# The starts of the stationary weights in the gate and up projections, moved chunk by chunk

## The chip, the cores and the metric

The kernel runs on one NeuronCore of one Trainium2 chip. Its time is the device time of one execution in microseconds. The time before is the median of three runs; a further execution was taken by the hardware profiler.

## What is computed

A decoder trunk of two layers over 256 tokens with a width of 1024, in float32. Each layer adds half of a SwiGLU FFN, a mixer, and half of a second FFN, each behind an RMS norm:

```python
def swiglu(x, w_gate, w_up, w_down):
    return (jax.nn.silu(x @ w_gate) * (x @ w_up)) @ w_down

for layer in range(DEPTH):          # 2
    h = h + 0.5 * swiglu(rms_norm(h, ffn1_norm[layer]), ...)
    hn = rms_norm(h, mix_norm[layer])
    h = h + (ab_mixer(hn, ...) if layer % 2 == 0 else c_mixer(hn, ...))
    h = h + 0.5 * swiglu(rms_norm(h, ffn2_norm[layer]), ...)
return rms_norm(h, final_norm)
```

The FFNs' inner width is 2816. The mixer of layer 0 is dilated window attention beside a spatial gate, that of layer 1 block-sparse attention. There are thus four FFNs, called the first to the fourth here; in the code they are phases 0, 2, 3 and 5, and phases 1 and 4 are the mixers.

## The kernel before

**Two parts of every number.** All large matrix products run in the type `F32R`. Each operand is split into its copy in that type and the rest that the copy lost, `whi` and `wlo` for weights, `xTh` and `xTl` for activations, and each product takes three matmuls: high by high, high by low, low by high.

**The stream of weights.** All weight matrices are cut into chunks of 128 x 2048 numbers. `Stream` brings them in their order of use: `load_one` starts the DMA into a `raw` buffer (3 of them), `split_parts` makes `whi` on ScalarE (L74) and `wlo` on VectorE (L75), each in two halves of 1024, and `take` hands a chunk to TensorE. There are 4 buffers for each part. A buffer has 2112 columns (`CH + LINE`), 64 more than a chunk, so that a chunk may start up to 256 bytes further on: `shift` in `Stream.add` counts columns of 4 bytes. Before the change chunks that are 256 wide start at `SHIFT`, 16 columns or 64 bytes, all others at 0.

**Where the operands lie.** In the built program `xTh` and `xTl` start at 36352 and 44544 bytes within each partition, the `whi` buffers at 170752, 179200, 187648 and 196096, the `wlo` buffers at 136960, 145408, 153856 and 162304. All these are multiples of 256, and the spacers `EDGE` and `GAP` are there in the layout. Within a chunk, each step of k is 1024 bytes and each half of the width 512 bytes further on. So the start of a stationary operand, less that of its moving operand, has one residue modulo 256 for a whole chunk and part; the text calls this residue the *distance*. Before the change it is 64 bytes for every chunk of width 256.

**An FFN.** The first 512 columns of gate and up are made in four blocks with activations as the stationary operand (`rowwise`, L199 to L201). The other 2304 columns are made by `colwise`: chunks of 256 columns, gate and up in turn, 18 chunks in each FFN. Here a 128 x 128 piece of the weights is stationary, and the 256 tokens of the activations are moving:

```python
for k in range(KD):
    h, l = w[0][:, k, cs], w[1][:, k, cs]
    nc.tensor.matmul(p, h, xh, ...)   # L322
    nc.tensor.matmul(p, h, xl, ...)   # L323
    nc.tensor.matmul(p, l, xh, ...)   # L324
```

One chunk is 2 halves of 8 steps of k, 16 such triples or 48 matmuls; one FFN is 288 triples. Between the first and the second chunk `turn_all` puts four transposes (L447); after that nothing but these triples stands on TensorE until the last chunk. Then `project` (L339, L340, L343) multiplies by the down matrix, in chunks whose start is 0. The mixers use `colwise` too, between other work, with chunks that start at 64 bytes; their attention scores (L539, L540) have `q` as the stationary and `kh` or `kl` as the moving operand, all of which start on multiples of 256.

The order on each engine is the order in which the program issues its work, apart from the tile framework's placing; the DMAs of the weights are issued from SyncE's queue.

Of the kernel before, what the change touches and what calls it, by code (L numbers as in the profile page):

```python
# [11 lines left out]
F32R = mybir.dt.float32r  # L12
# [12 lines left out]
CH = 2048  # L25
# [4 lines left out]
HEAT0 = 14  # L30


LINE, SHIFT = 64, 16
EDGE, GAP = 56, 8


class Stream:
# [4 lines left out]
        self.specs, self.raws, self.parts = [], {}, {}  # L42
        self.loaded = self.split = self.done = self.next = 0

    def add(self, src, nk, w, shift=0):
        self.specs.append((src, nk, w, 2 if len(self.specs) < 4 else 1, shift))

    def load_one(self):
# [15 lines left out]
    def split_parts(self):  # L64
        j = self.split
        nc = self.nc
        _, nk, w, cuts, shift = self.specs[j]
        n = nk * w
        raw = self.raws.pop(j)
        hi, lo = (p.tile([128, CH + LINE], F32R, name=m)[:, shift : shift + n]  # L70
                  for p, m in ((self.hi_pool, "whi"), (self.lo_pool, "wlo")))
        h = n // (2 * cuts)
        for a in range(0, n, h):
            nc.scalar.activation(hi[:, a : a + h], raw[:, a : a + h], AF.Copy)  # L74
            nc.vector.tensor_sub(lo[:, a : a + h], raw[:, a : a + h], hi[:, a : a + h].bitcast(F32))  # L75
            yield
        self.parts[j] = tuple(t.rearrange("p (k c) -> p k c", k=nk) for t in (hi, lo))
        self.split += 1
# [25 lines left out]
def trunk(ctx: ExitStack, tc: tile.TileContext, a, out):  # L104
# [15 lines left out]
    st = Stream(nc, (raw_pool, hi_pool, lo_pool))  # L120


    def add_cols(m, c0, w):
        n = CH // w
        for k in range(0, KD, n):
            st.add(m[k * 128 : (k + n) * 128, c0 : c0 + w], n, w, SHIFT if w == 256 else 0)

    def add_ffn(wg, wu, wd):
        for m in (wg, wu):
            add_cols(m, 0, 512)  # L130
        for c in range(512, FF, 256):
            for m in (wg, wu):
                add_cols(m, c, 256)
        add_rows(wd, range(0, FT, 2))

    def add_rows(m, order):
        for k in order:
            st.add(m[k * 128 : (k + 2) * 128, :], 2, D)

    add_ffn(a["ffn1_w_gate"][0], a["ffn1_w_up"][0], a["ffn1_w_down"][0])  # L140
    wab = a["ab_w_in"][0]
    add_cols(wab, 1024, 512)
    add_cols(wab, 2048, 512)
    add_cols(wab, 1536, 256)
    add_cols(wab, 1792, 256)
    for c in range(2):
        add_cols(wab, c * 256, 256)
        add_cols(wab, 512 + c * 256, 256)
    add_rows(a["ab_w_out"][0], (4, 6, 0, 2))
    add_ffn(a["ffn2_w_gate"][0], a["ffn2_w_up"][0], a["ffn2_w_down"][0])  # L150
    add_ffn(a["ffn1_w_gate"][1], a["ffn1_w_up"][1], a["ffn1_w_down"][1])
    wc = a["c_w_in"][0]
    add_cols(wc, 2048, 512)
    for c in range(4):
# [2 lines left out]
        add_cols(wc, c * 256, 256)  # L157
        add_cols(wc, 1024 + c * 256, 256)
    add_rows(a["c_w_out"][0], (0, 2, 4, 6))
    add_ffn(a["ffn2_w_gate"][1], a["ffn2_w_up"][1], a["ffn2_w_down"][1])  # L160


    def rows(v, n):
# [52 lines left out]
    class Norm:  # L216
# [8 lines left out]
        def add(self, h, bank, factor):  # L225
            sl = slice(h * 512, (h + 1) * 512)
            xs = xr[self.t][:, sl]
            if factor == 1.0:
                nc.vector.tensor_add(xs, bank, xs)
            else:  # L230
                nc.vector.scalar_tensor_tensor(xs, bank, factor, xs, op0=ALU.mult, op1=ALU.add)
# [578 lines left out]
```

## Time and profile before

| | before |
|---|---|
| runs, us | 962.03, 962.15, 965.7 (median 962.15) |
| profiled execution, us | 965.49 |
| its span, us | 963.8 |
| mean granted TensorE clock | 0.999 |
| TensorE matmuls busy, us | 951.3 (99%) |
| weight loads busy, us | 867.0 (90%) |
| VectorE busy, us | 560.6 (58%) |
| ScalarE busy, us | 523.1 (54%) |

The profiled execution is near the slowest of the three timed runs. Matmuls are pipelined, so the time that one matmul is shown with (276 ns for 256 columns) is longer than the distance from its start to the next one's; what a matmul costs is read from starts, or from counts over a stretch of time. In the names of a row, the output stands before the arrow and the operands behind it; `whi<-raw` is a split, `bank<-xTh,whi` a matmul into a PSUM bank.

### The profile page before, as it was taken

To read this page: it belongs to the slowest core of one execution; us is meant where nothing else is said; L and a number is where in the kernel's file an instruction comes from. 1 tells how busy PE (TensorE), PEld (TensorE's weight loads), DVE (VectorE), ACT (ScalarE), POOL (GpSimd) and SP (SyncE) were. 2 spreads that over 40 slices of the span, in tenths; PEclk is the share of its full clock that TensorE was granted. 3 is DMA by queue.
4 is the path that set the end of the run, shared out by engine and by line. 5 is a ranking of instruction groups with operands and counts; after the bars stand their busy time and mean duration, and the time that the engine had idled before them with its cause. 6 is when DMAs were issued, how large, how long until landed. Compare 5 with 4: busy or idle time off the path is not lost.

```text
span 963.8 us, 15449 instructions
## 1 busy us (share of the span) xinstructions
PE 951.3 (99%) x6371; PEld 867.0 (90%) x6371; DVE 560.6 (58%) x815; ACT 523.1 (54%) x875; POOL 42.0 (4%) x72
## 2 busy tenths in 40 slices
PE   9999999999999999999999999999999999999997
PEld 7999998889978999988789999888999779999885
DVE  6655544478766555454655555446788666555442
ACT  7644443476976444443654454337798775454431
POOL 0000000011200000000000000000213000000000
PEclk9999999999999999999999999999999999999999
DMA  9756555556334755555466565554543337565521
GB/s 323 246 176 204 190 186 207 175 173 223 128 130 159 234 176 179 195 195 180 154 211 198 182 212 177 202 190 142 178 170 132 131 113 259 187 206 179 208 96 44
DMA packets 119783, 174.70 MB, mean 181 GB/s; under 512 B 3952, under 2 KB 92832, under 8 KB 119712
## 3 DMA queue, kind: packets, MB, share of 16 engines
q1 hardware_dynamic: 117136, 171.48, 53.1%
q10 hardware_dynamic: 2576, 2.23, 0.8%
q8 instruction: 50, 0.82, 0.3%
q14 instruction: 21, 0.17, 0.1%
HBM read 172.65 MB, written 1.05 MB: 180 GB/s over the span
## 4 chain that ended last, share of the span: by engine, by line
PE 83%; ACT 7%; DVE 5%; issue 3%; POOL 1%; DMA 0%; POOLq 0%; SPq 0%; DVEq 0%; ACTq 0%
PE bank L322 15%; PE bank L324 15%; PE bank L323 15%; PE bank L339 9%; PE bank L343 9%; PE bank L340 9%; PE bank L199 4%; PE bank L200 4%; PE bank L201 4%; ACT whi L74 2%; DVE wlo L75 2%; ACT pr L545 1%; POOL rstd L211 1%; ACT pr L551 1%; DVE xTl L289 1%
## 5 line engine op out<-in xcount | busy, mean ns | idle before, releaser
L74 ACT ACTIVATE whi<-raw 128x1024 fp32r<-128x1024 f32 (+1 forms) x332 | 328.9, 1038 | 361.9 <-issue 230.6
L75 DVE TENSOR_TENSOR wlo<-raw,whi 128x1024 fp32r<-128x1024 f32 (+1 forms) x332 | 384.3, 1196 | 233.1 <-ACT whi L74 232.4
L322 PE MATMUL bank<-xTh,whi 128*128 128x256 f32 x1376 | 383.1, 279 | 0.0
L324 PE MATMUL bank<-xTh,wlo 128*128 128x256 f32 x1376 | 382.0, 278 | 0.0
L323 PE MATMUL bank<-xTl,whi 128*128 128x256 f32 x1376 | 382.0, 278 | 0.0
L324 PEld LDWEIGHTS bank<-xTh,wlo 128*128 128x128 f32 x1376 | 259.6, 189 | 0.1
L323 PEld LDWEIGHTS bank<-xTl,whi 128*128 128x128 f32 x1376 | 258.8, 188 | 0.2
L322 PEld LDWEIGHTS bank<-xTh,whi 128*128 128x128 f32 x1376 | 258.5, 188 | 0.3
L339 PE MATMUL bank<-whi,hTh 128*128 128x512 f32 x352 | 137.3, 390 | 0.0
L340 PE MATMUL bank<-wlo,hTh 128*128 128x512 f32 x352 | 137.0, 389 | 0.0
L343 PE MATMUL bank<-whi,hTl 128*128 128x512 f32 x352 | 113.7, 389 | 0.0
L438 DVE TENSOR_TENSOR hm<-sil,bank 128x512 f32<-128x512 f32 x44 | 30.2, 687 | 88.5 <-PE bank L324 78.2
L343 PEld LDWEIGHTS bank<-whi,hTl 128*128 128x128 f32 x352 | 66.1, 188 | 13.7
L340 PEld LDWEIGHTS bank<-wlo,hTh 128*128 128x128 f32 x352 | 66.1, 188 | 13.6
L339 PEld LDWEIGHTS bank<-whi,hTh 128*128 128x128 f32 x352 | 66.1, 188 | 13.5
L199 PE MATMUL bank<-whi,xTh 128*128 128x512 f32 x192 | 76.2, 397 | 0.1
L200 PE MATMUL bank<-wlo,xTh 128*128 128x512 f32 x192 | 75.4, 392 | 0.6 <-DVE wlo L75 0.5
L201 PE MATMUL bank<-whi,xTl 128*128 128x512 f32 x192 | 75.1, 391 | 0.0
L211 POOL TENSOR_TENSOR rstd<-ms,half_neg 128x1 f32<-128x1 f32 x14 | 12.9, 921 | 800.3 <-DVE ms L240 800.3
L200 PEld LDWEIGHTS bank<-wlo,xTh 128*128 128x128 f32 x192 | 36.1, 188 | 9.4 <-DVE wlo L75 2.5
L201 PEld LDWEIGHTS bank<-whi,xTl 128*128 128x128 f32 x192 | 36.0, 188 | 7.6
L199 PEld LDWEIGHTS bank<-whi,xTh 128*128 128x128 f32 x192 | 36.1, 188 | 7.4 <-ACT xTh L287 0.3
(91 smaller groups left out, 681.3 us busy)
## 6 DMA issues: line engine op xcount, KB each, us to landing
raw<-in_ffn_w_down SPq DMA_DIRECT2D x44, 1024.0 KB, 4.9
raw<-in_ffn_w_gate SPq DMA_DIRECT2D x42, 1024.0 KB, 5.2
raw<-in_ffn_w_up SPq DMA_DIRECT2D x42, 1024.0 KB, 5.3
raw<-in_c_w_in SPq DMA_DIRECT2D x12, 1024.0 KB, 5.2
raw<-in_ab_w_in SPq DMA_DIRECT2D x10, 1024.0 KB, 5.3
raw<-in_ab_w_out SPq DMA_DIRECT2D x4, 1024.0 KB, 5.0
raw<-in_c_w_out SPq DMA_DIRECT2D x4, 1024.0 KB, 4.8
raw<-in_ffn_w_gate SPq DMA_DIRECT2D x4, 512.0 KB, 6.5
```

The source lines that it names most:

```text
L74: nc.scalar.activation(hi[:, a : a + h], raw[:, a : a + h], AF.Copy)
L75: nc.vector.tensor_sub(lo[:, a : a + h], raw[:, a : a + h], hi[:, a : a + h].bitcast(F32))
L199: nc.tensor.matmul(p, sh, mh, start=start, stop=False)
L200: nc.tensor.matmul(p, sh, ml, start=False, stop=False)
L201: nc.tensor.matmul(p, sl, mh, start=False, stop=stop)
L322: nc.tensor.matmul(p, h, xh, start=k == 0, stop=False)
L323: nc.tensor.matmul(p, h, xl, start=False, stop=False)
L324: nc.tensor.matmul(p, l, xh, start=False, stop=k == KD - 1)
L339: nc.tensor.matmul(banks[t, h], sh, w[0][:, kw, cs], start=first, stop=False)
L340: nc.tensor.matmul(banks[t, h], sh, w[1][:, kw, cs], start=False, stop=False)
L343: nc.tensor.matmul(banks[t, h], sl, w[0][:, kw, cs], start=False, stop=last)
L438: nc.vector.tensor_mul(hm, g, pu)
```

## The change

Only the place of weight chunks inside their buffers is changed, and only for the 256-wide chunks of the four FFNs. `shift` becomes a pair, one number for `whi` and one for `wlo`. A new function `places` gives the pair for chunk `c` (0 to 17) of each FFN: `a` is a multiple of 16 bytes, 16 x (7c mod 16) in the first, third and fourth FFN and 16 x (5c mod 16) in the second, so that the chunks of an FFN pass through all 16 multiples under 256 and then repeat the first two. In the first and second FFN both parts are put at `a`; in the third `whi` stays at 64 bytes and `wlo` is put at `a`; in the fourth `whi` is put at `a` and `wlo` stays. The distances in the first, third and fourth FFN are thus, in units of 16 bytes, 0, 7, 14, 5, 12, 3, 10, 1, 8, 15, 6, 13, 4, 11, 2, 9, 0, 7, and in the second 0, 5, 10, 15, 4, 9, 14, 3, 8, 13, 2, 7, 12, 1, 6, 11, 0, 5; 4 is the distance before. The mixers' chunks stay at 64 bytes, all others at 0. Buffers keep their size and place.

```diff
+def places(ffn, c):
+    a = 4 * ((7, 5, 7, 7)[ffn] * c % 16)
+    return ((a, a), (a, a), (SHIFT, a), (a, SHIFT))[ffn]
...
-    def add(self, src, nk, w, shift=0):
+    def add(self, src, nk, w, shift=(0, 0)):
...
-        hi, lo = (p.tile([128, CH + LINE], F32R, name=m)[:, shift : shift + n]
-                  for p, m in ((self.hi_pool, "whi"), (self.lo_pool, "wlo")))
+        hi, lo = (p.tile([128, CH + LINE], F32R, name=m)[:, d : d + n]
+                  for p, m, d in ((self.hi_pool, "whi", shift[0]), (self.lo_pool, "wlo", shift[1])))
...
-    def add_cols(m, c0, w):
+    def add_cols(m, c0, w, shift=None):
         n = CH // w
         for k in range(0, KD, n):
-            st.add(m[k * 128 : (k + n) * 128, c0 : c0 + w], n, w, SHIFT if w == 256 else 0)
-
-    def add_ffn(wg, wu, wd):
+            st.add(m[k * 128 : (k + n) * 128, c0 : c0 + w], n, w, shift or ((SHIFT, SHIFT) if w == 256 else (0, 0)))
+
+    def add_ffn(i, wg, wu, wd):
         for m in (wg, wu):
             add_cols(m, 0, 512)
         for c in range(512, FF, 256):
-            for m in (wg, wu):
-                add_cols(m, c, 256)
+            for j, m in enumerate((wg, wu)):
+                add_cols(m, c, 256, places(i, (c - 512) // 128 + j))
         add_rows(wd, range(0, FT, 2))
```

The four calls of `add_ffn` pass 0 to 3 as the FFN's number.

More of the change, by code (lines that the diff above doesn't have):

```diff
@@ L138, in add_rows @@
             st.add(m[k * 128 : (k + 2) * 128, :], 2, D)
-    add_ffn(a["ffn1_w_gate"][0], a["ffn1_w_up"][0], a["ffn1_w_down"][0])
+    add_ffn(0, a["ffn1_w_gate"][0], a["ffn1_w_up"][0], a["ffn1_w_down"][0])
     wab = a["ab_w_in"][0]
@@ L149, in trunk @@
     add_rows(a["ab_w_out"][0], (4, 6, 0, 2))
-    add_ffn(a["ffn2_w_gate"][0], a["ffn2_w_up"][0], a["ffn2_w_down"][0])
-    add_ffn(a["ffn1_w_gate"][1], a["ffn1_w_up"][1], a["ffn1_w_down"][1])
+    add_ffn(1, a["ffn2_w_gate"][0], a["ffn2_w_up"][0], a["ffn2_w_down"][0])
+    add_ffn(2, a["ffn1_w_gate"][1], a["ffn1_w_up"][1], a["ffn1_w_down"][1])
     wc = a["c_w_in"][0]
@@ L159, in trunk @@
     add_rows(a["c_w_out"][0], (0, 2, 4, 6))
-    add_ffn(a["ffn2_w_gate"][1], a["ffn2_w_up"][1], a["ffn2_w_down"][1])
+    add_ffn(3, a["ffn2_w_gate"][1], a["ffn2_w_up"][1], a["ffn2_w_down"][1])
     def rows(v, n):
```

## The prediction

> **What bounds the kernel now.** I read the head of the page first, then the chain that ended last.
>
> ```profile
> span 963.8 us, 15449 instructions
> ...
> PE 951.3 (99%) x6371; PEld 867.0 (90%) x6371; DVE 560.6 (58%) x815; ACT 523.1 (54%) x875; POOL 42.0 (4%) x72
> ...
> PE 83%; ACT 7%; DVE 5%; issue 3%; POOL 1%; DMA 0%; POOLq 0%; SPq 0%; DVEq 0%; ACTq 0%
> ```
>
> TensorE is busy in 99% of the span, and the chain lies on it for 83%. No instruction is added or removed by the change, so the time can move only if single matmuls, or the splits that feed them, become longer or shorter. The profiled execution took 965.49 us for its span of 963.8 us; the three timed runs gave 962.03, 962.15 and 965.7.
>
> Next I compared stretches of the same work by counts: four stretches of 50 us, one in each FFN's `colwise` loop. Behind the stretch and its length stand each engine's busy time with its instructions (TensorE's matmuls, its weight loads, VectorE, ScalarE, GpSimd), then the granted clock, the DMA share and GB/s.
>
> ```profile
> 50.00:100.00 50.00, 50.00 (x444) 50.00 (x443) 26.42 (x27) 22.59 (x27) 0.00 (x0) 1.00 0.59 192
> 330.00:380.00 50.00, 50.00 (x427) 50.00 (x426) 26.40 (x26) 21.99 (x27) 0.00 (x0) 1.00 0.57 183
> 530.00:580.00 50.00, 50.00 (x444) 50.00 (x443) 28.13 (x29) 22.62 (x27) 0.00 (x0) 1.00 0.58 190
> 830.00:880.00 50.00, 50.00 (x444) 50.00 (x443) 27.77 (x29) 22.62 (x27) 0.00 (x0) 1.00 0.58 190
> ```
>
> The same loop does 444 matmuls in 50 us in three FFNs and only 427 in the second, at the same granted clock (1.00) and with PE busy throughout. So one and the same instruction has two lengths. The order of time shows them; a triple (L322, L323, L324) is one step of k.
>
> ```profile
> 60.49 0.28 PE L322 MATMUL bank<-xTh,whi 128*128 128x256 f32 x1
> ...
> 63.55 0.28 PE L322 MATMUL bank<-xTh,whi 128*128 128x256 f32 x1
> ...
> 340.59 0.28 PE L322 MATMUL bank<-xTh,whi 128*128 128x256 f32 x1
> ...
> 343.77 0.28 PE L322 MATMUL bank<-xTh,whi 128*128 128x256 f32 x1
> ```
>
> Nine triples lie between each pair: 3.06 us or 340 ns a triple in the first FFN (113.3 a matmul), 3.18 us or 353.3 ns in the second (117.8). I call these the low and the high level; they differ by 13.3 ns a triple. In both stretches the stationary operand starts 64 bytes behind the moving one, counted modulo 256, so at this distance both levels are possible. The line's own view, asked for each FFN from the restart after its first chunk to the end of its loop, shows how firmly a level is held (minimum, median and maximum of one matmul in ns; in the order first to fourth FFN):
>
> ```profile
> L322 PE MATMUL bank<-xTh,whi x271: 276/276/276, 40.8 to 132.6; 128*128 128x256 f32 x136
> L322 PE MATMUL bank<-xTh,whi x271: 281/281/281, 318.3 to 413.7; 128*128 128x256 f32 x136
> L322 PE MATMUL bank<-xTh,whi x270: 276/276/276, 505.9 to 597.3; 128*128 128x256 f32 x135
> L322 PE MATMUL bank<-xTh,whi x270: 276/276/276, 805.4 to 896.9; 128*128 128x256 f32 x135
> ```
>
> Each FFN has one level for some 90 us, 276 or 281 ns in a matmul's own duration. It is drawn where four transposes (L447) interrupt the loop, once in each FFN, after the first chunk; that chunk was on the high level in all four. The first chunk of the third FFN, and the restart:
>
> ```profile
> L322 PE MATMUL bank<-xTh,whi x15: 281/281/281, 499.4 to 504.4; 128*128 128x256 f32 x15
> 504.81 0.49 PE L447 MATMUL bank<-ident,hm 128*128 128x128 f32 x3
> ```
>
> I read this as two stable timings between the weight load and the running matmul, chosen by a few nanoseconds at the restart and then kept. Whether distance matters as well is told by the score matmuls (L539, L540), whose operands both start on a multiple of 256: distance 0, the same 256 columns.
>
> ```profile
> 246.84 0.28 PE L539 MATMUL bank<-kh,q 128*128 128x256 f32 x1
> ...
> 247.80 0.28 PE L322 MATMUL bank<-xTh,whi 128*128 128x256 f32 x1
> ...
> 248.16 0.28 PE L322 MATMUL bank<-xTh,whi 128*128 128x256 f32 x1
> ...
> 733.10 0.28 PE L322 MATMUL bank<-xTh,whi 128*128 128x256 f32 x1
> 733.44 0.28 PE L539 MATMUL bank<-kh,q 128*128 128x256 f32 x1
> ...
> 733.80 0.28 PE L540 MATMUL bank<-kl,q 128*128 128x256 f32 x1
> ```
>
> Eight score matmuls take 0.96 us (120 ns each). At 733 they follow a triple of 0.34 us and are at 0.12 at once: distance 0 leaves the low level whatever came before. And the triple after the eight takes 0.36 us: back at distance 64, without a stop, the high level is kept.
>
> **The change part by part.** On every engine the instructions stand in the same order with the same shapes, and all buffers lie where they lay; the DMA queue and its landings are untouched. What moves is the start of a stationary operand, by a multiple of 16 bytes: in the first two FFNs for `whi` and `wlo` of 17 of the 18 chunks (816 of 864 matmuls each), in the third for `wlo` alone (272), in the fourth for `whi` alone (544); 2448 of 3456 matmuls.
>
> *The splits.* ScalarE writes `whi` and VectorE reads it and writes `wlo` at the new starts. I cost this at nothing.
>
> ```profile
> L75 DVE TENSOR_TENSOR wlo<-raw,whi 128x1024 fp32r<-128x1024 f32 x38 | 44.8, 1221 | 24.9 <-ACT whi L74 24.9
> L74 ACT ACTIVATE whi<-raw 128x1024 fp32r<-128x1024 f32 x36 | 36.2, 1054 | 51.1 <-issue 44.0 <-PE bank L323 5.8 <-DMA raw<-in_ffn_w_up 1.4
> ```
>
> These are the groups of the first FFN's loop (34 to 133 us). A chunk is 16 triples, 5.44 us of TensorE; its splits are 2 x 1.054 on ScalarE and 2 x 1.221 on VectorE. In the 50 us stretches VectorE is busy 26 to 28 us, ScalarE 23. The cover of about 2.4 us a chunk is gone only if a split took twice as long.
>
> *The matmuls.* First the floor. In the profiled run the high level holds in the second FFN (288 triples) and in the first chunk of each other FFN (16 triples each, before the transposes): 336 x 13.3 ns = 4.5 us. With all FFNs low this execution would take 961.0 us. It stands 3.3 us over the median; the second FFN low from its restart would take 272 x 13.3 ns = 3.6 us off, so I take the two faster timed runs for the same program with that FFN settled low. The floor holds for both.
>
> All 1152 FFN triples high cost 15.4 us over the floor. In the other direction no row goes below the low level. At distance 0, 20 ns a triple over the low level is paid instead of 13.3: four chunks with both parts there and four with one, at most 0.8 us more, taken as 0.4.
>
> What share of the triples will be high? Before, each FFN drew its level once. After, there is a new distance every 5.4 us; each FFN passes distance 0 in its first chunk and again in its seventeenth (one operand of two in the last two FFNs), and distance 0 drops TensorE to the high side. Between lies only the one restart after the first chunk. The nearest rows are the mixers, where the same loop at distance 64 is entered again and again from scores and transposes. Mean durations of L323 by stage, in the order first FFN, second FFN, dilated mixer (216 to 255 us), block-sparse mixer (666 to 741):
>
> ```profile
> L323 PE MATMUL bank<-xTl,whi 128*128 128x256 f32 x288 | 79.6, 276 | 0.0
> L323 PE MATMUL bank<-xTl,whi 128*128 128x256 f32 x288 | 80.9, 281 | 0.0
> L323 PE MATMUL bank<-xTl,whi 128*128 128x256 f32 x95 | 26.4, 278 | 0.0
> L323 PE MATMUL bank<-xTl,whi 128*128 128x256 f32 x128 | 35.7, 280 | 0.0
> ```
>
> 276 is all low, 281 all high, so the mixers stand at 0.4 and 0.8, weighted (95 x 0.4 + 128 x 0.8)/223 = 0.63. I take that share for the disturbed FFN loops: 0.63 x 15.4 = 9.7 us. The bounds are 0 (every distance but 0 lets the drawn level stand) and 1 (one bad distance is enough, and nothing releases). Sum: 961.0 + 9.7 + 0.4 = 971.1, forecast 971 us.
>
> A rule of the Trainium skill speaks against all of this: its page "TensorE: Matmul & The Clock Gate", Part 2 (Step-by-step), says that TensorE has two independent read ports, so that loading the next weights takes nothing from the running matmul. By that rule the distance would be without effect and the time would stay near 962. The trace disagrees: 120 ns at distance 0 against 113.3 at 64, same columns, same clock.
>
> **The rivals.**
> 1. *The drawn level survives.* Distances other than 0 may be as neutral as 64, each FFN settles at its restart (three of four settled low in this profile) and keeps the level through sixteen chunks. For it: inside an FFN no switch of chunk changes anything before, though buffers rotate. Against it: the residue never changed there, and after 120 ns at distance 0 the high level stayed. With under 0.38 of the triples high: 961 to 966.9, so not slower by more than the bound. The rule of the two ports belongs here.
> 2. *Nothing releases.* The first bad distance puts each FFN on the high level to its end. For it: 247.80 to 248.16 above. Against: the mixers do come back, at transposes. 961.0 + 15.4 + 0.4 = 976.8; I count 975.2 to 978 to it.
> 3. *Some distances are dearer than 0.* No row shows more than 120 ns for a steady run of 256 columns, but no row has a start off a multiple of 32 either. If half the chunks paid twice the excess of distance 0 (126.7 ns, 40 ns a triple), 576 x 40 ns = 23 us, with the rest at 0.63 x 7.7 = 4.8: 989.
> 4. *Some distances are better than 64: faster.* From 0 to 64 6.7 ns went; were another 4.4 ns a matmul to go in half the chunks, 1728 x 4.4 ns = 7.6 us would leave 953.4. It decides from 0.27 of the time (961.0 to 957.3 is 3.7 us, over 15.2). Against it speak the 512-column rows:
>
> ```profile
> 146.99 0.39 PE L339 MATMUL bank<-whi,hTh 128*128 128x512 f32 x1
> 147.22 0.39 PE L340 MATMUL bank<-wlo,hTh 128*128 128x512 f32 x1
> ```
>
> 0.23 us from start to start for 512 columns, twice the low level's 0.113 for 256, though one weight load of the same 128 columns now has double the time beside it: 113.3 looks like what 256 columns cost undisturbed. The same page of the Trainium skill (Back-to-back issue gap) gives 262 cycles for 256 columns, 109.2 ns as an estimate at its 2.4 GHz; no run here shows that for this type.
>
> **How the numbers follow.** The forecast's case, a mixed share of 0.4 to 0.9 (967.1 to 975.2), has 0.42; rival 1 has 0.25, rival 2 0.20, rival 3 0.10, rival 4 0.03. A measurement of this kernel tells about 0.5% from no change, 4.8 us of 962.15: faster means under 957.3, slower over 967.0. So slower 0.42 + 0.20 + 0.10 = 0.72, same 0.25, faster 0.03. The range takes in rivals 1 and 2 down to the floor and up to the dearest sum: 961 to 978, leaving out 0.13.
>
> **What would show it right or wrong.** Right: starts of L322 that step by 340 ns in some chunks and 353 to 360 in others, changing at borders of chunks; the first and the seventeenth chunk of the first two FFNs at 360; splits of L74 and L75 still near 1054 and 1221 ns; chain on PE as before. Rival 1: 444 matmuls in 50 us in most FFNs. Rival 2: 427 or fewer in all four. Wrong altogether: steps under 340 or over 360 ns, a split twice as long, or idle time of PE ahead of L322 with `whi` or `wlo` as releaser.

## The result: 978.12 us, 1.4% slower, and the profile after

The changed kernel takes 978.12 us (median of four runs, 978.05 to 978.15), where the kernel before took 963.92 (median of four, 962.03, 962.15, 965.7 and 969.46). The ratio is 1.0143, 95% interval 1.0109 to 1.0176. The forecast was 971, the range 961 to 978, so the time lies at its upper end, 0.1 us past it. The profiled execution took 978.14 us for a span of 976.4 us; before it was 965.49 for 963.8, so 12.6 us came in.

The head of the page after, and its chain that ended last:

```profile
span 976.4 us, 15449 instructions
...
PE 963.9 (99%) x6371; PEld 879.5 (90%) x6371; DVE 560.9 (57%) x815; ACT 523.8 (54%) x875; POOL 42.0 (4%) x72
...
PE 87%; DVE 4%; ACT 4%; issue 3%; POOL 1%; DMA 0%; POOLq 0%; SPq 0%; DVEq 0%; ACTq 0%
```

TensorE's busy time went from 951.3 to 963.9 us, by the 12.6 us of the span; VectorE and ScalarE stand where they stood. Stretches of 50 us within the four `colwise` loops (the columns are as in the prediction):

```profile
50.00:100.00 50.00, 50.00 (x425) 50.00 (x424) 25.80 (x27) 22.45 (x27) 0.00 (x0) 1.00 0.60 189
335.00:385.00 50.00, 50.00 (x427) 50.00 (x426) 26.41 (x26) 21.65 (x28) 0.00 (x0) 1.00 0.60 183
530.00:580.00 50.00, 50.00 (x428) 50.00 (x427) 26.33 (x27) 22.29 (x27) 0.00 (x0) 1.00 0.61 190
830.00:880.00 50.00, 50.00 (x427) 50.00 (x427) 27.70 (x28) 22.64 (x27) 0.00 (x0) 1.00 0.60 189
```

Before, the counts were 444, 427, 444 and 444; now all four FFNs, at 425 to 428, are within two of the second one's. From start to start, the 864 matmuls of each FFN's loop add up to 98.2, 101.8, 98.2 and 98.2 us before and to 102.4, 102.3, 101.9 and 102.2 after: 12.4 of the 12.6 us. The mixers' `colwise` work, which was not changed, is at 79.2 and 79.3 us.

The splits, the groups of the whole kernel, which have moved lines (L74 and L75 are L81 and L82 now, and L322 to L324 are L329 to L331):

```profile
L82 DVE TENSOR_TENSOR wlo<-raw,whi 128x1024 fp32r<-128x1024 f32 x316 | 374.3, 1223 | 237.4 <-ACT whi L81 236.7
L81 ACT ACTIVATE whi<-raw 128x1024 fp32r<-128x1024 f32 x316 | 320.2, 1059 | 373.8 <-issue 241.6 <-PE bank L350 75.7 <-PE bank L330 28.2
```

1223 and 1059 ns: the new starts cost the splits nothing.

What the loss looks like inside an FFN is seen at chunk 12 of the first, the one that lies at 64 bytes as before, between chunk 11 (208 bytes) and chunk 13 (176 bytes). The line's own view for each of the three (minimum, median and maximum of one matmul):

```profile
L329 PE MATMUL bank<-xTh,whi x16: 276/278/279, 97.5 to 102.8; 128*128 128x256 f32 x16
L329 PE MATMUL bank<-xTh,whi x16: 276/276/287, 103.1 to 108.3; 128*128 128x256 f32 x16
L329 PE MATMUL bank<-xTh,whi x16: 278/279/283, 108.6 to 113.9; 128*128 128x256 f32 x16
```

Only chunk 12 has a median of 276 ns, the low level. By starts, the triples of these chunks take 350, 340 and 355 ns. Over all 72 chunks of the four FFNs, four run at 340: three with both parts at 64 bytes, and the one with `whi` at 64 and `wlo` at 192. The others lie between 347 and 367 ns, each with its own step; the mean over all is 355.

### The profile page after: what moved, and what is told of

It is laid out like the page before. It is cut to its first block, busy times and chain, and to the rows that moved or that the text cites. A ratio compares the mean times of both kernels' runs of the same rounds, so it can differ in the third digit from the quotient of the medians.

```text
span 976.4 us, 15449 instructions
## 1 busy us (share of the span) xinstructions
PE 963.9 (99%) x6371; PEld 879.5 (90%) x6371; DVE 560.9 (57%) x815; ACT 523.8 (54%) x875; POOL 42.0 (4%) x72
## 4 chain that ended last, share of the span: by engine, by line
PE 87%; DVE 4%; ACT 4%; issue 3%; POOL 1%; DMA 0%; POOLq 0%; SPq 0%; DVEq 0%; ACTq 0%
PE bank L330 16%; PE bank L329 16%; PE bank L331 16%; PE bank L346 9%; PE bank L350 9%; PE bank L347 9%; PE bank L206 4%; PE bank L207 4%; PE bank L208 4%; DVE wlo L82 1%; POOL rstd L218 1%; ACT whi L81 1%; DVE xTl L296 1%; ACT xn L262 1%; PE bank L284 1%
## 5 line engine op out<-in xcount | busy, mean ns | idle before, releaser
L81 ACT ACTIVATE whi<-raw 128x1024 fp32r<-128x1024 f32 (+1 forms) x332 | 329.3, 1040 | 373.8 <-issue 241.6
L82 DVE TENSOR_TENSOR wlo<-raw,whi 128x1024 fp32r<-128x1024 f32 (+1 forms) x332 | 384.4, 1197 | 238.3 <-ACT whi L81 237.5
L329 PE MATMUL bank<-xTh,whi 128*128 128x256 f32 x1376 | 386.8, 281 | 0.0
L330 PE MATMUL bank<-xTl,whi 128*128 128x256 f32 x1376 | 386.2, 281 | 0.0
L331 PE MATMUL bank<-xTh,wlo 128*128 128x256 f32 x1376 | 385.9, 281 | 0.0
L329 PEld LDWEIGHTS bank<-xTh,whi 128*128 128x128 f32 x1376 | 259.4, 189 | 0.3
L331 PEld LDWEIGHTS bank<-xTh,wlo 128*128 128x128 f32 x1376 | 259.6, 189 | 0.1
```

The lines of the kernel that those rows point to most:

```text
L329: nc.tensor.matmul(p, h, xh, start=k == 0, stop=False)
L330: nc.tensor.matmul(p, h, xl, start=False, stop=False)
L331: nc.tensor.matmul(p, l, xh, start=False, stop=k == KD - 1)
```

## The experiments

Steps below are nanoseconds per triple, from start to start of the matmuls in the trace (340 is the low level, 353 the prediction's high level). The fences show stretches of equal length, one in each FFN from the first to the fourth unless the text says otherwise; in 40 us some 356 matmuls mean a step of 340, 342 a step of 353, 336 a step of 360. A step given for an FFN or a chunk is a mean where single triples differ: at 56 bytes, for one, triples of 348 to 360 ns take turns. A pair such as (64, 192), or 64 with 192, gives the places of `whi` and `wlo` in bytes. All but the two kernels that are given with intervals ran once.

**One distance for a whole FFN.** In `places`:

```diff
-    a = 4 * ((7, 5, 7, 7)[ffn] * c % 16)
-    return ((a, a), (a, a), (SHIFT, a), (a, SHIFT))[ffn]
+    a = (48, 56, 32, 52)[ffn]
+    return a, a
```

> Both parts of all 18 chunks of an FFN at one distance, with no change inside an FFN: 192, 224, 128 and 208 bytes in the first to fourth FFN. Theory M (memory: a bad distance puts TensorE on the high level and it stays there): a constant distance other than 0 is as neutral as 64, so after the restart behind the first chunk each FFN settles at 340 ns a triple in about three cases of four; the time is 962 to 966 us. Theory D (each distance has its own step, whatever came before): the same steps as these distances had inside the changed kernel, 353, 350, 355 to 360 and 350 ns, held through the whole FFN; 288 triples each, 13 + 10 + 17 + 10 ns above 340, together about 14 us over the floor of 961: 974 to 976 us.

```profile
90.00:130.00 40.00, 40.00 (x342) 40.00 (x341) 21.69 (x22) 17.60 (x21) 0.00 (x0) 1.00 0.55 184
370.00:410.00 40.00, 40.00 (x345) 40.00 (x345) 21.77 (x23) 17.61 (x21) 0.00 (x0) 1.00 0.55 185
550.00:590.00 40.00, 40.00 (x340) 40.00 (x338) 21.12 (x22) 17.72 (x23) 0.00 (x0) 1.00 0.56 187
850.00:890.00 40.00, 40.00 (x345) 40.00 (x345) 21.70 (x22) 17.58 (x21) 0.00 (x0) 1.00 0.57 186
```

975.43 us. The steps are 353, 350, 356 and 350, much as in the changed kernel, from the restart to the end of each FFN. No FFN settled at 340. So a distance has a step of its own, and the change of distance from chunk to chunk is not what costs.

**The low part alone.** `whi` stays at 64 bytes:

```diff
+    return SHIFT, (48, 32, 20, 0)[ffn]
```

> The high part whi stays at 64 bytes everywhere; wlo of all chunks of an FFN lies at one distance: 192, 128, 80 and 0 bytes in the first to fourth FFN. Theory M: 340 after the restart in most FFNs, 962 to 966 us. Theory D: as in the third FFN of the changed kernel, 340 at 192, 355 at 128, 353 at 80; at 0 that kernel had 353 in its first chunk and 367 in its seventeenth, so there the start decides as well. Time 961 + 0 + 4.3 + 3.7 + 3.7 to 7.8: 972 to 977 us.

```profile
85.00:125.00 40.00, 40.00 (x355) 40.00 (x354) 22.89 (x23) 19.11 (x24) 0.00 (x0) 1.00 0.58 198
370.00:410.00 40.00, 40.00 (x340) 40.00 (x339) 21.00 (x22) 17.88 (x23) 0.00 (x0) 1.00 0.57 187
550.00:590.00 40.00, 40.00 (x342) 40.00 (x341) 20.40 (x20) 17.55 (x21) 0.00 (x0) 1.00 0.56 185
850.00:890.00 40.00, 40.00 (x342) 40.00 (x341) 21.43 (x22) 18.01 (x23) 0.00 (x0) 1.00 0.56 188
```

972.91 us; 340, 355, 353 and 353. One matmul in three uses `wlo`, and yet its place alone costs a triple 13 to 15 ns in three FFNs: at 128 as much as both parts there (355 against 356 in the run before), at 80 and 0 less than both parts did in the changed kernel (356 to 357, and 360). With `wlo` at 192 the first FFN is at 340 from its third triple on, which 64 with 64 was not before the restart in any profile here.

**Everything moved, distances kept.** The kernel before with both spacers changed:

```diff
-EDGE, GAP = 56, 8
+EDGE, GAP = 40, 24
```

> The kernel before with every operand of its matmuls moved by 64 bytes (activations and weight buffers alike), so that all distances stay and all places change: stationary weights of the 256-wide chunks lie at 128 modulo 256, moving activations at 64. If the step hangs on the difference of the two places alone (theory D and theory M both): the same as before, 962 to 966 us, with FFNs at 340 and now and then 353 ns. If it hangs on the place of the stationary operand itself (theory P): 128 is a bad place, 354 to 360 ns in all four FFNs, 976 to 984 us.

Two stretches, in the second and the fourth FFN:

```profile
360.00:400.00 40.00, 40.00 (x356) 40.00 (x355) 20.87 (x21) 17.56 (x21) 0.00 (x0) 1.00 0.57 187
840.00:880.00 40.00, 40.00 (x355) 40.00 (x355) 22.65 (x24) 19.53 (x24) 0.00 (x0) 1.00 0.59 203
```

961.83 us (eight runs, 961.62 to 962.04). Weights at 128 modulo 256 are in no bad place when the activations lie at 64. Beside it the kernel before gave 14 times, on the same chip, five runs from 961.77 to 961.99 and nine from 965.25 to 965.66; the ratio is 0.9973 (0.9959 to 0.9987). The 3.6 us between the two groups are what the prediction took for one FFN on the high level, and 969.46 above is twice that over 962. Why this kernel drew the low level in all of its runs and the kernel before in five of fourteen is open.

**Activations moved, weights left.** The counterpart: the weights of the 256-wide chunks stay in their place, and the moving operand goes to meet them.

```diff
-EDGE, GAP = 56, 8
+EDGE, GAP = 56, 24
...
-            st.add(m[k * 128 : (k + n) * 128, c0 : c0 + w], n, w, SHIFT if w == 256 else 0)
+            st.add(m[k * 128 : (k + n) * 128, c0 : c0 + w], n, w, SHIFT)
...
-            st.add(m[k * 128 : (k + 2) * 128, :], 2, D)
+            st.add(m[k * 128 : (k + 2) * 128, :], 2, D, SHIFT)
```

> The kernel before, with the activations (and all that is allocated behind them) moved by 64 bytes and the 256-wide weight chunks left where they were, 64 modulo 256; the other chunks are moved by 64 too, so that their distances stay 0. The distance of the 256-wide chunks becomes 0 with the weights in their good place. If the difference of the places decides: 360 ns a triple in all four FFNs and the mixers, as with weights at 0 and activations at 0: 961.0 plus 1152 x 20 ns = 23 us, plus about 3 in the mixers: 985 to 987 us. If the place of the weights alone decides: 962 to 966 us.

The same two FFNs:

```profile
360.00:400.00 40.00, 40.00 (x336) 40.00 (x335) 20.65 (x21) 17.23 (x22) 0.00 (x0) 1.00 0.56 182
840.00:880.00 40.00, 40.00 (x336) 40.00 (x335) 20.62 (x21) 17.55 (x21) 0.00 (x0) 1.00 0.58 184
```

984.98 us, and 360 ns in every chunk of the FFNs and in nearly all triples of the mixers. With the run before it this shows, for a move of 64 bytes, that the difference between the two operands' places decides, not the place of either. The splits, which write into the same buffers beside the matmuls, are no rival cause: in the first FFN of this run the 111 triples during which VectorE was busy throughout and the 109 during which it stood idle all average 360 ns, and so it is with ScalarE; in the first FFN of the kernel before both kinds of triples stand at 340.

**64 for one part, 192 for the other, everywhere.** In the FFNs and the mixers:

```diff
+    return SHIFT, 48
...
-            st.add(..., shift or ((SHIFT, SHIFT) if w == 256 else (0, 0)))
+            st.add(..., shift or ((SHIFT, 48) if w == 256 else (0, 0)))
```

> All 256-wide chunks, those of the mixers too, with whi at 64 and wlo at 192 bytes. In the changed kernel this pair went from a 354 ns chunk to 340 within two triples, without a stop, while 64 with 64 remained at 353 once (third FFN, chunk 12). Theory D, with this pair having only the low step: 340 from the first chunk of each FFN on and in the mixers; the floor of 961.0 less 64 triples of first chunks (0.9 us) and less the high groups of the mixers (some 15 groups of 8 triples, 1.6 us): 958 to 960 us in every run, without a spread of 3.6 us between runs. Theory M: no better than 64 with 64, levels drawn per FFN, 962 to 966 us.

The second and fourth FFN, and the first chunk of the first and of the second FFN:

```profile
360.00:400.00 40.00, 40.00 (x356) 40.00 (x355) 20.73 (x22) 18.01 (x22) 0.00 (x0) 1.00 0.56 194
840.00:880.00 40.00, 40.00 (x356) 40.00 (x355) 22.92 (x23) 18.62 (x23) 0.00 (x0) 1.00 0.58 193
```

```profile
L328 PE MATMUL bank<-xTh,whi x16: 276/276/281, 34.5 to 39.7; 128*128 128x256 f32 x16
L328 PE MATMUL bank<-xTh,whi x16: 276/276/281, 311.9 to 317.0; 128*128 128x256 f32 x16
```

961.11 us (seven runs, 961.0 to 961.27), 0.9967 of the kernel before (0.9950 to 0.9984), and better than both kernels; against the five low runs of the kernel before (961.77 to 961.99) it gains some 0.8 us. All FFNs are low from their first chunk on, in the mixers all but some interrupted stretches, and no level is left to be drawn. It is above the 958 to 960 that was expected. The floor of 961.0 already had the first chunks low (they are among its 336 triples), so their 0.9 us was taken off twice, and the mixers gave less than the 1.6 put down for them: `colwise` work is 392.2 us in the FFNs and 78.5 in the mixers here, against 392.9 and 79.2 in the profile of the kernel with everything moved, which drew low four times. So 0.7 and 0.7 us were there to be had over that kernel, and 0.7 of these 1.4 arrived in the median; where the rest went is open.

**A few bytes beside 64.** Both parts at 56, 60, 68 and 72 bytes:

```diff
+    a = (14, 15, 17, 18)[ffn]
+    return a, a
```

> Both parts of all chunks of an FFN near the good distance: 56, 60, 68 and 72 bytes in the first to fourth FFN (before: 64; in the changed kernel 48 and 80 gave 354 and 356 ns a triple). Theory L (what counts are lines of 16 bytes: a start off a multiple of 16 behaves like its line, or worse, since each load then touches one line more): 56 and 60 like 48, 68 and 72 like 64 or dearer: 354, 354, 340 to 356, 340 to 356. Theory W (a window in time around 64: a few bytes shift the load by a few columns' time against the moving operand, and the loss grows smoothly): 60 and 68 near 340 to 345, 56 and 72 between that and 355. Time 961 to 976 us.

```profile
90.00:130.00 40.00, 40.00 (x342) 40.00 (x341) 21.70 (x22) 17.60 (x21) 0.00 (x0) 1.00 0.57 185
370.00:410.00 40.00, 40.00 (x337) 40.00 (x337) 20.85 (x22) 17.40 (x22) 0.00 (x0) 1.00 0.58 185
550.00:590.00 40.00, 40.00 (x340) 40.00 (x339) 21.70 (x22) 17.59 (x21) 0.00 (x0) 1.00 0.59 186
850.00:890.00 40.00, 40.00 (x341) 40.00 (x340) 21.34 (x22) 17.79 (x23) 0.00 (x0) 1.00 0.60 189
```

978.87 us, above the range expected; 353, 358, 355 and 355. Theory W falls: one number of 4 bytes to either side already costs 15 ns or more. Theory L is not refuted: 56 is near the 355 that 48 had in the changed kernel, the two above 64 are dearer, and 60, at 358, is covered only by its "or worse". That lines of 16 bytes are the reason is not shown.

**Is it the 128 bytes between the parts?**

```diff
+    return ((48, 16), (0, 32), (32, 0), (16, 48))[ffn]
```

> The pairs (whi, wlo) at (192, 64), (0, 128), (128, 0) and, as the control, (64, 192) bytes in the first to fourth FFN: always 128 bytes between the two parts. Theory R (what makes 64 with 192 good is that the two parts lie 128 apart): 340 ns a triple in all four, 961 to 962 us. Theory D (each load pairs with the moving operand, and only 64 is good for whi): above 350 in the first three, as 192 for whi alone gave 357 in the changed kernel and 0 gave 353, and 340 in the fourth: 971 to 977 us.

```profile
85.00:125.00 40.00, 40.00 (x355) 40.00 (x354) 22.91 (x23) 19.11 (x24) 0.00 (x0) 1.00 0.61 200
370.00:410.00 40.00, 40.00 (x338) 40.00 (x337) 21.27 (x22) 17.63 (x22) 0.00 (x0) 1.00 0.57 185
550.00:590.00 40.00, 40.00 (x340) 40.00 (x339) 20.58 (x21) 17.55 (x21) 0.00 (x0) 1.00 0.57 184
850.00:890.00 40.00, 40.00 (x356) 40.00 (x355) 22.30 (x23) 17.94 (x22) 0.00 (x0) 1.00 0.57 188
```

970.39 us; 340, 358, 355, 340. Neither theory holds whole. 128 between the parts is not enough, but 192 with 64 is as good as 64 with 192, although the changed kernel had 356 there (fourth FFN, chunk 4). One pair with two steps suggests that what came before counts after all; the next run tests it.

**Entered late.** Chunks 0 to 8 at a dear pair, then a pair that had shown 340:

```diff
+    first = ((0, 0), (0, 0), (0, 0), (20, 16))[ffn]
+    return first if c < 9 else ((48, 16), (16, 48), (16, 16), (48, 16))[ffn]
```

> Chunks 0 to 8 of each FFN lie at a dear pair (whi, wlo), chunks 9 to 17 at a pair that ran at 340 ns a triple elsewhere, entered without a stop: (0, 0) then (192, 64); (0, 0) then (64, 192); (0, 0) then (64, 64); (80, 64) then (192, 64) bytes. In the changed kernel (192, 64) had 357 in one chunk that followed (80, 64), and as the only pair of an FFN it has 340. Theory D (the pair alone decides): 340 from chunk 9 on in all four, about 968 us. Theory H (what came before decides where a pair has two steps): 357 from chunk 9 on in the fourth FFN, and perhaps in the first; (64, 64) either 340 or 353; (64, 192) at 340: 969 to 973 us.

The second half of each FFN, 35 us, in which 311 matmuls mean a step of 340, 300 one of 353 and 297 one of 357:

```profile
95.00:130.00 35.00, 35.00 (x311) 35.00 (x310) 19.29 (x20) 15.08 (x18) 0.00 (x0) 1.00 0.53 181
...
370.00:405.00 35.00, 35.00 (x311) 35.00 (x311) 18.30 (x19) 15.09 (x19) 0.00 (x0) 1.00 0.56 184
...
560.00:595.00 35.00, 35.00 (x300) 35.00 (x299) 19.11 (x20) 16.14 (x20) 0.00 (x0) 1.00 0.55 190
...
865.00:900.00 35.00, 35.00 (x297) 35.00 (x296) 18.79 (x20) 15.07 (x18) 0.00 (x0) 1.00 0.54 181
```

975.71 us (the expectation's sums were too low, the steps are what tells). 192 with 64 gets to 340 out of the 360 of distance 0, and stays at 357 for nine chunks out of the 353 of (80, 64). 64 with 64, out of distance 0, stays at 353 for nine chunks. This is theory H: the pair decides which steps there are, the entry which of them is taken, and while the pair stays and nothing stops it the step stays. Each of these entries was run once.

**All at 192.**

```diff
+    return 48, 48
```

> Both parts at 192 bytes in all four FFNs. One FFN with it stood at 353 ns a triple from end to end. Theory B (period of 128 bytes: 192 is as 64, with two steps drawn at the restart): some FFNs at 340, 962 to 973 us. Theory O (192 with 192 has only the high step): 353 in all four, 961 less 0.9 for no change in the first chunks, plus 15.4: 976 us.

The second and fourth FFN:

```profile
370.00:410.00 40.00, 40.00 (x342) 40.00 (x341) 21.42 (x22) 17.61 (x21) 0.00 (x0) 1.00 0.55 185
850.00:890.00 40.00, 40.00 (x342) 40.00 (x342) 21.68 (x22) 17.59 (x21) 0.00 (x0) 1.00 0.56 185
```

976.38 us, 353 in all four FFNs, as theory O had it. But the next run shows 340 for the same pair, so O is too strong.

**Two pairs in turn.** The pair changes with every chunk:

```diff
+    return (((16, 48), (48, 16)), ((16, 16), (16, 48)), ((16, 16), (48, 48)), ((16, 48), (0, 0)))[ffn][c % 2]
```

> The pair (whi, wlo) changes with every chunk, between two pairs: first FFN (64, 192) and (192, 64), second (64, 64) and (64, 192), third (64, 64) and (192, 192), fourth (64, 192) and (0, 0) bytes. Theory N (a change of place costs nothing by itself): 340 throughout in the first and second FFN, 340 and 353 or only 353 in the third, 340 and 360 by chunk in the fourth. Theory K (each change of place is a kick that can leave the matmuls on a high step): above 340 in many chunks of the first and second FFN. Time by N: 960.5 to 961.5 plus 2 to 3.6 for the third and 2.9 for the fourth: 965.5 to 968 us; by K some 970 us or more.

```profile
85.00:125.00 40.00, 40.00 (x356) 40.00 (x354) 22.91 (x23) 19.10 (x24) 0.00 (x0) 1.00 0.58 197
360.00:400.00 40.00, 40.00 (x355) 40.00 (x355) 20.72 (x22) 17.93 (x22) 0.00 (x0) 1.00 0.59 191
540.00:580.00 40.00, 40.00 (x356) 40.00 (x355) 22.63 (x23) 19.51 (x24) 0.00 (x0) 1.00 0.61 204
840.00:880.00 40.00, 40.00 (x346) 40.00 (x346) 21.69 (x22) 18.08 (x22) 0.00 (x0) 1.00 0.58 189
```

964.67 us, 0.8 us under the sum by theory N, since the third FFN was low but for its first two chunks. A change of place costs nothing by itself: 340 in all chunks of the first FFN, and after the first chunks in the second and third. In the third, 64 with 64 comes to 340 in chunk 2 without a stop, out of 192 with 192 at 353, and from then on 192 with 192 runs at 340 too, entered from 64 with 64 on the low level. In the fourth the chunks alternate, 340 and 360, back and forth: distance 0 takes its 360 and 64 with 192 returns to 340 each time.

**The long matmuls.** The good pair for all 256-wide chunks, and the down matrices, moving operands of 512 columns, at 0, 64, 128 and 192 bytes:

```diff
+        a = (0, 16, 32, 48)[i]
-        add_rows(wd, range(0, FT, 2))
+        add_rows(wd, range(0, FT, 2), (a, a))
```

> The kernel with whi at 64 and wlo at 192 bytes in all 256-wide chunks (961.1 us), with the chunks of the four down matrices, which are the moving operand of 512-column matmuls there, moved by 0, 64, 128 and 192 bytes in the first to fourth FFN. Each weight load of 128 columns stands beside 512 moving columns, so it has double the time. Theory S (slack: distance costs only where the load is as long as the matmul): 227 ns a matmul at all four, 961 us. Theory C (each load collides with the running matmul's reads and costs the same nanoseconds whatever the length): up to 5 to 7 ns more for 264 matmuls in each of the three moved FFNs, 4 to 5.5 us: 965 to 967 us.

40 us of each down projection:

```profile
140.00:180.00 40.00, 40.00 (x178) 33.15 (x177) 18.37 (x16) 14.52 (x15) 0.00 (x0) 1.00 0.58 190
417.00:457.00 40.00, 40.00 (x177) 32.81 (x176) 18.12 (x16) 14.84 (x15) 0.00 (x0) 1.00 0.58 194
600.00:640.00 40.00, 40.00 (x174) 32.44 (x173) 16.70 (x15) 15.08 (x16) 0.00 (x0) 1.00 0.58 193
900.00:940.00 40.00, 40.00 (x173) 32.25 (x172) 16.53 (x14) 14.07 (x14) 0.00 (x0) 1.00 0.37 130
```

964.35 us against 961.1. From start to start the mean is 227 ns at distance 0 and 2, 5.4 and 6.5 ns more in the three moved ones; in the kernel with the good pair and no down matrix moved all four are at 227. Slack does not absorb it: theory S falls, and C is near in size (a little below its 965 to 967). That it is a collision of reads, as C has it, is not shown. Here, with 512 columns, distance 0 is the best of the four.

## Where the prediction was right, and where its sum was off

*The direction and the place* were right: 12.4 of the 12.6 us are in the `colwise` matmuls of the four FFNs, at the same clock, with TensorE busy throughout; the splits stayed at 1059 and 1223 ns, and no wait for `whi` or `wlo` ended a stretch of the chain there.

*Two timings, drawn at the restart and kept* was right for 64 with 64: the runs of the kernel before fall into groups 3.6 us apart, the 272 x 13.3 ns of one FFN, and the profile that the prediction was made from was one with the second FFN high.

*The term that failed is the share.* I took 0.63 of the triples to be high, from the mixers, which all lie at 64 bytes: they show how often a disturbed loop returns to the low level where the distance allows one. Of the distances that the change brings in, hardly any does. Only 4 chunks of 72 were low, and the rest not at one high level but at 347 to 367 ns. The loops are 408.9 us together; with all triples low they are 392.2 (64 with 192). So the change costs 16.7 us over the floor, where the sum had 9.7 + 0.4.

*Rival 2* had the nearest time, 976.8, by a mechanism that the runs do not bear out. "Nothing releases" is wrong: in the changed kernel 64 with 64 came back to 340 without a stop in three of four cases, once out of a chunk at 359. It stayed at 353 in the fourth, so memory is real, but a minor part in the changed kernel. *Rival 1*, the drawn level surviving, fell with the runs of one distance each. Its rule, the two independent read ports of the Trainium skill ("TensorE: Matmul & The Clock Gate", Part 2, Step-by-step), would have the time unchanged; moving the activations by 64 bytes, with the weights where they were, brought 360 instead of 340 ns, so here the two operands do not leave each other alone. That their reads hinder each other is the reading at hand, and no trace shows the reads. *Rival 3* had something: 367 ns was seen in one chunk, and steps of 362, over the 360 of distance 0, but nothing near the 380 that it was priced with. *Rival 4* fell: no FFN and no chunk had a step below 340 in any run; the better version gains by holding 340 in all FFNs.

*Expected of the profile after:* chunks 0 and 16 of the first two FFNs at 360, as foretold, and changes at the borders of chunks. Steps over 360, named as a sign of error, did occur.

What is not settled is why a pair has the steps it has. The difference of places decides, 4 bytes matter, and one part alone makes the whole triple dear; which reads meet, the trace does not show.

## What to carry to other kernels

In a kernel like this one, where `F32R` matmuls stand back to back for most of the time, the difference of the two operands' start places is worth trying as a tuning parameter: between the best and the worst setting tried here lie 24 us of 961, or 2.5%. Try several, with the two operands of a split product at different ones, and compare counts of matmuls in equal stretches at equal clock. A loop that runs at another speed in one execution than in the next, or in one stage than in another of the same shape, can be a sign that its place allows two timings; look for a place that allows only the better one. Price a scan over unknown settings from rows at other settings, not from how often the present one recovers.

## What the runs showed of the hardware that was not expected

- A triple of 128 x 128 by 256 columns takes 340 ns at the best pairs of distances and 360 at distance 0, and with both parts at 60 bytes instead of 64 it takes 358.
- The same instructions at the same places hold 340 or 353 ns for 90 us, by how the loop was entered; (192, 64) holds 340 or 357, (192, 192) 340 or 353.
- Matmuls of 512 columns, which give the weight load twice the time, lose up to 6.5 ns each when the place of their weights is moved, and the best of the four distances tried is 0, where 256 columns pay 360 ns a triple.
